# Neighbourhood attention with the transposed probabilities as stationary operand, and division by the denominators after the weighing

## Chip, core and metric

The kernel runs on one core of a Trainium2 chip. The metric is the device time of one execution in microseconds; the time before is the median of three runs. TensorE (PE) multiplies, with a separate record for its loads of stationary data (PEld); VectorE (DVE), ScalarE (ACT) and GpSimd (POOL) do the elementwise work; SyncE (SP) issues most of the transfers.

## What is computed

One layer of a hybrid encoder: an input projection, a state-space mixer, a neighbourhood attention over a 16 x 64 grid of tokens, an output projection and an MLP, all in float32. The change touches the attention alone. Cut to it, the reference is:

```python
def neighbourhood_attention(q, k, v, q_norm_w, k_norm_w, rpb):
    ...
    s = jnp.einsum("bjhd,bajchd->bhjac", q_i, k_win) + bias
    p = jax.nn.softmax(s.reshape(bsz, NA_HEADS, GRID_W, kh * NA_COLS), axis=-1)
    ...
    return jnp.einsum("bhjac,bajchd->bjhd", p, v_win)
...
x = x + jnp.concatenate([y_ssm, y_na], axis=-1) @ w_out
```

There are 1024 tokens, 16 heads of 64 dimensions, and a window of 8 rows by 16 columns.

## The kernel before

The tokens are put in 8 blocks of 128 (16 rows by 8 columns), so that the window of a block of queries lies in its own block of keys and the two beside it. Float32 products are made of halves: a value is split into a high part in fp32r and a remainder, and products of the parts are summed.

The attention runs over 8 pairs of heads, and in a pair over two heads (`attend`). For each of the 8 blocks b of queries it does this:

- Two matmuls (lines 931 and 934) put the scores of the block against up to three key blocks in a PSUM bank (`psc`, of two). q is stationary, with its high and low part stacked in the partitions; k moves, 256 or 384 columns.
- One DVE instruction (line 939) adds the bias with the mask (`mb`) and gives the row's maximum (`nmx`). ACT takes the exponential and sums it into the denominator `den` (line 949).
- DVE takes the reciprocal of the denominator (line 957) and multiplies the row by it (line 958).
- PE transposes the two or three pieces of 128x128 (line 962) into a bank `ptp` (of two), and ACT and DVE split them into `pth` and `ptl` (lines 184 and 185, `split_from_psum`).
- Three blocks later, `weigh(g)` multiplies key block g: v of that block, with its high and low part side by side (128 columns), is stationary, and the transposed probabilities of up to three query blocks move (line 908). Query blocks 0 to 3 sum into bank `pv0`, 4 to 7 into `pv1`. There are 20 such matmuls a head: 8 of 384 columns, 8 of 256, 4 of 128.
- After the last one of a bank, ACT copies the lower half of its partitions into the grid order (`yT`, line 918), and DVE adds the upper half (line 919).

After a pair, `yT` (128 dimensions by 1024 tokens) is stored to `na_dr` (line 996). At the start of the last pair, three earlier pairs are loaded again and split (lines 986 to 991); the last pair's output is split from `yT` itself (line 999).

Between the blocks stand fillers: the output projection of three quarters of its inner dimension (`w_out_part`, lines 178 to 180 as `po`), in pieces of 12 matmuls of 512 columns, about one for three blocks. Their weights are split by ACT (line 148) and POOL (line 149). POOL also builds the bias tile of each head (line 881). The instructions of an engine run in the order in which a scheduler has put them; so do the transfers that SP issues.

Of the kernel before, what the change touches and what calls it, by code (L numbers as in the profile page):

```python
# [1 line left out]

# [1 line left out]

# [51 lines left out]
def hymba_block(  # L56
# [135 lines left out]
    def to_grid(dst, h):  # L192
        v = dst.rearrange("p (i b j) -> p b i j", b=8, j=8)
        return v[:, 4 * h : 4 * h + 4]

    def from_blocks(src):
        return src.rearrange("p (b i j) -> p b i j", b=4, j=8)
# [575 lines left out]
    with ExitStack() as ph:  # L773
# [18 lines left out]
        def w_out_part(part, yt):  # L792
            for f in range(4 * part + len(yt), 4 * part + 4):
                yl = yp.tile([P, T], F32R, tag="yl", name="yl", bufs=4)
                yh = yp.tile([P, T], F32R, tag="yh", name="yh", bufs=4)
                yf = yl.bitcast(F32)
                if f < 8:
                    nc.sync.dma_start(
                        yf.rearrange("p (c f) -> p c f", c=NT),
                        y_dr[:, :, f * P : (f + 1) * P].rearrange("c p f -> p c f"),  # L800
                    )
                    pts = []
                    for h in range(2):
                        pt = ps_tp("pty")
                        for j in range(4):
                            c = 4 * h + j
                            nc.tensor.transpose(
                                pt[:, j * P : (j + 1) * P], yf[:, c * P : (c + 1) * P], ident
                            )
                        pts.append(pt)  # L810
                    for h in range(2):
                        s = slice(h * 512, (h + 1) * 512)
                        split_from_psum(
                            yh[:, s], yl[:, s], pts[h], pcol[:, 72 + f : 73 + f]
                        )
                else:
                    nc.sync.dma_start(yf, na_dr[f - 8])
                    split_na(yh, yl, yf, nc.gpsimd)
                yt.append((yh, yl))
            for h, t in ((h, t) for h in range(2) for t in range(NT)):  # L820
                if t == 0:
                    get = load_w_nat(w_out[0], 512 * part, 4, 512 * h, nc.gpsimd)
                pt = ps_mm("po")
                s = slice(t * P, (t + 1) * P)
                for k in range(4):
                    yh, yl = yt[k]
                    mm3(pt, yh[:, s], yl[:, s], *get(k), k == 0, k == 3)
                d = x2[:, t, h * 512 : (h + 1) * 512]
                if part == 0:
                    nc.sync.dma_start(  # L830
                        d, x[0, t * P : (t + 1) * P, h * 512 : (h + 1) * 512]
                    )
                nc.vector.tensor_tensor(d, d, pt, op=add)
                yield
# [54 lines left out]
        pth = ap.tile([P, NT, 3, P], F32R, name="pth", bufs=1)  # L889
        ptl = ap.tile([P, NT, 3, P], F32R, name="ptl", bufs=1)  # L890

        def attend(hh, mb, q, k, kl, v, yT):
            hp = slice(HD * hh, HD * hh + HD)
            nmx = ap.tile([P, 8], F32, tag="nmx", name="nmx")
            den = ap.tile([P, 8], F32, tag="den", name="den")
            pv = [ps_v("pv0"), None]

            def weigh(g):
                b0, b1 = max(g - 1, 0), min(g + 2, NT)
                for i in range(2):  # L900
                    c0, c1 = max(b0, 4 * i), min(b1, 4 * i + 4)
                    if c0 >= c1:
                        continue
                    first, last = g == 3 * i, g == 4 + 3 * i
                    if first and i:
                        pv[1] = ps_v("pv1")
                    for pt in (pth, ptl):
                        pvm = nc.tensor.matmul(
                            pv[i][:, (c0 - 4 * i) * P : (c1 - 4 * i) * P],
                            lhsT=v[:, g, hh],  # L910
                            rhs=pt[:, g, c0 - g + 1 : c1 - g + 1, :],
                            start=first and pt is pth,
                            stop=last and pt is ptl,
                            skip_group_check=True,
                        )
                    if last:
                        yo = to_grid(yT[hp], i)
                        nc.scalar.copy(yo, from_blocks(pv[i][0:HD]))
                        nc.vector.tensor_tensor(
                            yo, yo, from_blocks(pv[i][HD:P]), op=add  # L920
                        )
                return pvm

            for b in range(NT):
                g0, g1 = max(b - 1, 0), min(b + 2, NT)
                m = g1 - g0
                n = m * P
                o = (3 if b == 0 else 5 if b == NT - 1 else 0) * P
                qs, ks = slice(b * P, (b + 1) * P), slice(g0 * P, g1 * P)
                pt = ps_s("psc")  # L930
                nc.tensor.matmul(
                    pt[:, 0:n], lhsT=q[:, hh, qs], rhs=k[:, hh, ks], start=True, stop=False
                )
                mark = nc.tensor.matmul(
                    pt[:, 0:n], lhsT=q[:, hh, qs], rhs=kl[:, hh, ks], start=False, stop=True
                )
                pr = ap.tile([P, 384], F32, tag="pr", name="pr", bufs=4)
                db = den[:, b : b + 1]
                nc.vector.tensor_tensor_reduce(  # L939
                    pr[:, 0:n],  # L940
                    pt[:, 0:n],
                    mb[:, o : o + n],
                    scale=-1.0,
                    scalar=3.0e38,
                    op0=add,
                    op1=ALU.min,
                    accum_out=nmx[:, b : b + 1],
                )
                nc.scalar.activation(
                    pr[:, 0:n],  # L950
                    pr[:, 0:n],
                    AF.Exp,
                    bias=nmx[:, b : b + 1],
                    scale=-1.0,
                    accum_out=db,
                )
                nc.vector.reciprocal(db, db)
                nc.vector.tensor_scalar(pr[:, 0:n], pr[:, 0:n], db, None, op0=mul)
                pp = ps_tp("ptp")
                for j in range(m):  # L960
                    s = slice(j * P, (j + 1) * P)
                    nc.tensor.transpose(pp[:, s], pr[:, s], ident)  # L962
                s0 = 2 * g0 + b + 1
                hi, lo = (
                    t.rearrange("p g s q -> p (g s) q")[:, s0 : s0 + 2 * m - 1 : 2, :]
                    for t in (pth, ptl)
                )
                pv3 = pp[:, 0:n].rearrange("p (j q) -> p j q", q=P)
                split_from_psum(hi, lo, pv3)
                if b > 2:  # L970
                    weigh(b - 3)
                done[0] += 1
                if done[0] * 44 // 128 > (done[0] - 1) * 44 // 128:
                    with tc.issue_after(mark.ins):
                        fill()
            weigh(NT - 3)
            weigh(NT - 2)
            return mark, weigh(NT - 1)

        filler += [w_out_part(0, []), w_out_part(1, []), w_out_part(2, [])]  # L980
        last = []
        fill(2)
        for p in range(8):
            q, k, kl, v = load_qkv(p)
            if p == 7:
                for j, tag in enumerate(("q", "k", "v")):
                    hl = b0.tile([P, 2, T], F32R, tag=tag, name="hl", bufs=1)
                    yf = hl[:, 1].bitcast(F32)
                    nc.sync.dma_start(yf, na_dr[4 + j])
                    split_na(hl[:, 0], hl[:, 1], yf, nc.gpsimd)  # L990
                    last.append((hl[:, 0], hl[:, 1]))
            yT = yt.tile([P, T], F32, tag="yT", name="yT", bufs=1)
            for hh in range(2):
                marks = attend(hh, bias_for(2 * p + hh), q, k, kl, v, yT)
            if p < 7:
                nc.sync.dma_start(na_dr[p], yT)
            else:
                hl = b0.tile([P, 2, T], F32R, tag="kl", name="hl", bufs=1)
                split_na(hl[:, 0], hl[:, 1], yT, nc.vector)
                last.append((hl[:, 0], hl[:, 1]))  # L1000
        for i in (0, 1):
            with tc.issue_after(marks[i].ins):
                fill()
# [391 lines left out]
```

## Time and profile before

| | |
|---|---|
| median of 3 runs | 1684.91 us |
| lowest, highest | 1677.66, 1690.37 us |
| profiled execution, span from first to last instruction | 1676.4 us |
| attention, first to last weighing matmul | 689.2 to 964.5 us |
| mean granted PE clock | 0.986 |

The profile describes one execution, and the span above is the time that it gives for that execution. A row of a group has the line, the engine, the operation, output and inputs, partitions x elements and the count; then the busy time in us and the mean of one in ns; then how long the engine stood idle just before, and what ended that. A row of the stretch table has the busy time of each engine between two times. In the order of time, a row has the start and the duration in us, and xN says that N instructions in a row are merged. A PE matmul's duration contains its way through the array; the next one starts before it ends.

### The profile page before, as it was taken

The numbers are of one execution on the slowest core, as the hardware profiler recorded it, in microseconds if no ns is written. First come the engines' busy times: TensorE is split into PE (matmuls) and PEld (weight loads), VectorE is DVE, ScalarE is ACT, GpSimd is POOL, SyncE is SP. The second block draws the span as 40 slices with busy tenths as digits, with TensorE's granted clock in tenths as the row PEclk, the third lists the DMA queues.
The fourth block names the chain that finished last, engine by engine and source line by source line (L and its number), as shares of the span: only waits on it lengthen the run. The fifth ranks groups of instructions, "written<-read, shape, count | busy, mean of one in ns | idle before, by whom it ended". The sixth has DMA issues, their size and how long they took to land. (4 is left out here: it accounts for less than half of the span.)

```text
span 1676.4 us, 20931 instructions
## 1 busy us (share of the span) xinstructions
PE 1590.8 (95%) x7453; PEld 1297.3 (77%) x7453; DVE 1106.0 (66%) x1686; ACT 721.3 (43%) x1187; POOL 708.4 (42%) x506
## 2 busy tenths in 40 slices
PE   6999999998988899998999989999999989999999
PEld 5788888777766678887778767788888868888887
DVE  5767214788796852888898867544243387887863
ACT  5434223434343442556565533554444444433330
POOL 4000003888687862322243232244444465455551
PEclk9999999999999999999999999999999989999999
DMA  8113337876666785956664141353344386644231
GB/s 217 51 38 105 93 100 212 215 194 196 229 220 173 218 263 190 281 165 185 180 190 118 62 164 50 101 201 126 138 164 150 127 295 231 216 149 151 101 101 75
DMA packets 178755, 269.75 MB, mean 161 GB/s; under 512 B 14219, under 2 KB 105307, under 8 KB 178651
## 3 DMA queue, kind: packets, MB, share of 16 engines
q1 hardware_dynamic: 134667, 227.51, 44.1%
q10 hardware_dynamic: 42976, 37.23, 7.3%
q0 software_dynamic: 1008, 3.67, 0.5%
q8 instruction: 59, 0.97, 0.3%
q14 instruction: 45, 0.37, 0.1%
HBM read 185.21 MB, written 86.50 MB: 162 GB/s over the span
## 5 line engine op out<-in xcount | busy, mean ns | idle before, releaser
L760 POOL TENSOR_TENSOR wl<-wraw,wh 128x1024 fp32r<-128x1024 f32 x110 | 298.5, 2724 | 318.4 <-ACT wh L759 297.1
L759 ACT ACTIVATE wh<-wraw 128x1024 fp32r<-128x1024 f32 x110 | 115.6, 1054 | 149.7 <-PE px L745 50.8
L745 PE MATMUL px<-wh,ahl 128*128 128x512 f32 x512 | 162.5, 395 | 3.3 <-ACT ahl L759 3.3
L179 PE MATMUL pq<-wl,hTh 128*128 128x512 f32 x384 | 153.6, 402 | 4.9 <-DVE wl L149 4.8
L178 PE MATMUL pq<-wh,hTh 128*128 128x512 f32 x384 | 154.4, 405 | 3.5 <-ACT wh L148 3.5
L745 PE MATMUL px<-h,wh 128*128 128x512 f32 x496 | 156.0, 396 | 1.4 <-DVE x L1078 1.4
L180 PE MATMUL pq<-wh,hTl 128*128 128x512 f32 x384 | 152.9, 399 | 0.0
L760 DVE TENSOR_TENSOR ahl<-ar,ahl 128x1024 fp32r<-128x1024 f32 x56 | 115.1, 2062 | 23.2 <-ACT ahl L759 22.1
L759 ACT ACTIVATE ahl<-ar 128x1024 fp32r<-128x1024 f32 x56 | 58.2, 1052 | 140.1 <-PE px L745 75.3
L745 PEld LDWEIGHTS px<-wh,ahl 128*128 128x128 f32 x512 | 97.0, 190 | 25.0 <-ACT ahl L759 3.7
L745 PEld LDWEIGHTS px<-h,wh 128*128 128x128 f32 x496 | 93.2, 188 | 24.0 <-ACT h L184 1.6
L149 DVE TENSOR_TENSOR wl<-wraw,wh 128x1024 fp32r<-128x1024 f32 x40 | 55.3, 1386 | 81.9 <-ACT wh L148 81.2
L745 PE MATMUL px<-wl,ahl 128*128 128x512 f32 x256 | 101.0, 395 | 0.0
L745 PE MATMUL px<-h,wl 128*128 128x512 f32 x248 | 98.1, 395 | 0.0
L881 POOL TENSOR_TENSOR mb<-braw,nam 128x256 f32<-128x256 f32 (+1 forms) x48 | 40.1, 863 | 131.1 <-DVE nmx L939 72.2
L179 PEld LDWEIGHTS pq<-wl,hTh 128*128 128x128 f32 x384 | 73.6, 192 | 23.1 <-DVE wl L149 8.6
L149 POOL TENSOR_TENSOR wl<-wraw,wh 128x1024 fp32r<-128x1024 f32 x18 | 43.0, 2401 | 110.5 <-ACT wh L148 110.5
L178 PEld LDWEIGHTS pq<-wh,hTh 128*128 128x128 f32 x384 | 74.0, 193 | 20.2 <-ACT wh L148 5.2
L184 ACT ACTIVATE pth<-ptp 128x384 fp32r<-128x384 f32 (+1 forms) x128 | 57.7, 455 | 73.1 <-PE ptp L962 72.5
L612 POOL TENSOR_TENSOR rb<-rb,c 128x512 f32<-128x512 f32 x64 | 77.0, 1223 | 20.4 <-DMA rb<-cum_dr 19.2
L180 PEld LDWEIGHTS pq<-wh,hTl 128*128 128x128 f32 x384 | 73.5, 191 | 15.0
L745 PE MATMUL pz<-h,wh 128*128 128x512 f32 x256 | 80.8, 396 | 0.8 <-DVE h L185 0.8
(268 smaller groups left out, 4211.4 us busy)
## 6 DMA issues: line engine op xcount, KB each, us to landing
ar<-act_dr SPq DMA_DIRECT2D x56, 512.0 KB, 3.7
act_dr<-cq SPq DMA_DIRECT2D x49, 512.0 KB, 3.2
wraw<-in_w_in_dram SPq DMA_DIRECT2D x44, 512.0 KB, 4.3
rb<-cum_dr SPq DMA_DIRECT2D x32, 512.0 KB, 7.2
wraw<-in_w_mlp_in_dram SPq DMA_DIRECT2D x32, 512.0 KB, 4.6
wraw<-in_w_mlp_out_dram SPq DMA_DIRECT2D x32, 512.0 KB, 5.2
q_dr<-hl ACTq DMA_DIRECT2D x64, 128.0 KB, 3.6
k_dr<-hl ACTq DMA_DIRECT2D x16, 512.0 KB, 5.3
```

Source lines behind the costliest of these rows:

```text
L149: lo_eng.tensor_tensor(lo[:, 0:n], raw[:, 0:n], hi[:, 0:n].bitcast(F32), op=sub)
L178: nc.tensor.matmul(pt, lhsT=ah, rhs=bh, start=first, stop=False)
L179: nc.tensor.matmul(pt, lhsT=ah, rhs=bl, start=False, stop=False)
L180: return nc.tensor.matmul(pt, lhsT=al, rhs=bh, start=False, stop=last)
L184: nc.scalar.activation(hi, src, AF.Copy)
L612: nc.gpsimd.tensor_tensor(rb[:, d], rb[:, d], c1[:, d, c, h0 : h0 + 4].unsqueeze(2).broadcast_to([P, 4, P]), op=sub,)
L745: nc.tensor.matmul(pt, lhsT=a, rhs=b, start=f, stop=l, skip_group_check=True)
L759: nc.scalar.activation(hl[0], src, AF.Copy)
L760: eng.tensor_tensor(hl[1], src, hl[0].bitcast(F32), op=sub)
L881: nc.gpsimd.tensor_tensor(mb[:, s].rearrange("p (s r c) -> p s r c", r=16, c=8), v[:, a:b], nam[:, s].rearrange("p (s r c) -> p s r c", r= ...
```

## The change

The operands of the weighing change places: a 128x128 piece of `pth` or `ptl` (keys by queries) is stationary, and v moves. For each pair of key block and query block there are two matmuls: `pth` with v's high and low part (128 columns), and `ptl` with v's high part alone (64 columns). A head has 22 such pairs, so 44 matmuls. The bank then holds queries by dimensions.

Since queries are now in the partitions, the probabilities are not normalised any more: the lines of the reciprocal and of the product are gone, and the output is divided. When a bank is complete, DVE takes the reciprocal of four denominators at once, ACT copies the part from v's low half out of PSUM, DVE adds the other, and POOL multiplies by the reciprocals into `yn` (queries by both heads of the pair). The part of `ptl` with v's low half was computed before and is not any more.

`turn_out` brings the pair's output back to dimensions by tokens: 8 transposes, and a copy by ACT for each four (for the last pair a split by ACT and DVE). It is called in block 3 of the next pair's first head, so the store to `na_dr` moves there too, and for the seventh pair the three loads and splits follow it. The scratch area of software DMA is set to 4096 bytes.

```diff
-                for i in range(2):
-                    c0, c1 = max(b0, 4 * i), min(b1, 4 * i + 4)
...
-                    for pt in (pth, ptl):
-                        pvm = nc.tensor.matmul(
-                            pv[i][:, (c0 - 4 * i) * P : (c1 - 4 * i) * P],
-                            lhsT=v[:, g, hh],
-                            rhs=pt[:, g, c0 - g + 1 : c1 - g + 1, :],
...
+                for c in range(b0, b1):
+                    i = c // 4
...
+                    nc.tensor.matmul(
+                        pv[i][:, c0 : c0 + P],
+                        lhsT=pth[:, g, c - g + 1, :],
+                        rhs=v[:, g, hh],
...
+                    pvm = nc.tensor.matmul(
+                        pv[i][:, c0 : c0 + HD],
+                        lhsT=ptl[:, g, c - g + 1, :],
+                        rhs=v[:, g, hh, 0:HD],
...
-                        yo = to_grid(yT[hp], i)
-                        nc.scalar.copy(yo, from_blocks(pv[i][0:HD]))
-                        nc.vector.tensor_tensor(
-                            yo, yo, from_blocks(pv[i][HD:P]), op=add
+                        parts = pv[i].rearrange("p (b a d) -> p b a d", a=2, d=HD)
+                        bs = slice(4 * i, 4 * i + 4)
+                        nc.vector.reciprocal(den[:, bs], den[:, bs])
+                        yo = ap.tile([P, 4, HD], F32, tag="yo", name="yo")
+                        nc.scalar.copy(yo, parts[:, :, 1])
+                        nc.vector.tensor_tensor(yo, yo, parts[:, :, 0], op=add)
+                        nc.gpsimd.tensor_tensor(
+                            yn[:, bs, hh],
+                            yo,
+                            den[:, bs].unsqueeze(2).broadcast_to([P, 4, HD]),
+                            op=mul,
                         )
...
-                nc.vector.reciprocal(db, db)
-                nc.vector.tensor_scalar(pr[:, 0:n], pr[:, 0:n], db, None, op0=mul)
...
+                if b == 3 and late:
+                    late.pop()()
...
+        def turn_out(p, yn):
+            yf = hl = None
+            if p < 7:
+                yf = yt.tile([P, T], F32, tag="yT", name="yT", bufs=1)
+            else:
+                hl = b0.tile([P, 2, T], F32R, tag="kl", name="hl", bufs=1)
+            for h in range(2):
+                pt = ps_tp("pty")
+                for j in range(4):
+                    nc.tensor.transpose(
+                        pt[:, j * P : (j + 1) * P],
+                        yn[:, 4 * h + j].rearrange("p a d -> p (a d)"),
+                        ident,
+                    )
+                if p < 7:
+                    nc.scalar.copy(to_grid(yf, h), from_blocks(pt))
+                else:
+                    hi, lo = to_grid(hl[:, 0], h), to_grid(hl[:, 1], h)
+                    split_from_psum(hi, lo, from_blocks(pt))
+            if p < 7:
+                nc.sync.dma_start(na_dr[p], yf)
+            else:
+                last.append((hl[:, 0], hl[:, 1]))
+            if p == 6:
...
+            yn = yt.tile([P, NT, 2, HD], F32, tag="yn", name="yn", bufs=1)
             for hh in range(2):
-                marks = attend(hh, bias_for(2 * p + hh), q, k, kl, v, yT)
...
+            late.append(partial(turn_out, p, yn))
+        late.pop()()
...
+    nc = bacc.Bacc(
+        "TRN2", target_bir_lowering=False, num_devices=1, dynamic_dma_scratch_size=4096
+    )
```

Since lines were added, the changed kernel's lines have other numbers; in `attend` 931, 934, 939 and 962 are now 945, 948, 953 and 974, and earlier in the file each is one higher (184 and 185 are 185 and 186, 881 is 882). The order is seen at two places. The first is PE in the first head, in the blocks between two fillers; `psc` are the scores, `ptp` the transposes, `pv` the weighing. Before:

```order
L962 MATMUL ptp<-ident,pr 128x128 x3
L908 MATMUL pv_5598<-ptl,v 128x256
L908 MATMUL pv_5598<-pth,v 128x384
L962 MATMUL ptp<-ident,pr 128x128 x3
L908 MATMUL pv_5598<-ptl,v 128x384
L908 MATMUL pv_5598<-pth,v 128x384
L931 MATMUL psc<-k,q 128x384
L934 MATMUL psc<-kl,q 128x384
```

And in the changed kernel:

```order
L974 MATMUL ptp<-ident,pr 128x128 x3
L915 MATMUL pv_5598<-v,ptl 128x64
L907 MATMUL pv_5598<-v,pth 128x128
L915 MATMUL pv_5598<-v,ptl 128x64
L907 MATMUL pv_5598<-v,pth 128x128
L915 MATMUL pv_5598<-v,ptl 128x64
L907 MATMUL pv_5598<-v,pth 128x128
L945 MATMUL psc<-k,q 128x384
L948 MATMUL psc<-kl,q 128x384
```

Where one or two long matmuls stood between transposes and scores, a run of six short ones stands, each with stationary data of its own.

The second place is DVE in the same head, around the completion of the first bank. Before:

```order
L958 TENSOR_SCALAR pr<-pr,den 128x256
L957 RECIPROCAL den<-den 128x1
L185 TENSOR_TENSOR ptl<-ptp,pth 128x3x128
L958 TENSOR_SCALAR pr<-pr,den 128x256
L939 ISA pr,nmx<-psc,mb 128x384
L939 ISA nmx 128x1
L919 TENSOR_TENSOR yT<-yT,pv_5598 64x4x16x8
```

And in the changed kernel:

```order
L926 RECIPROCAL den<-den 128x4
L834 TENSOR_TENSOR x_5441<-x_5441,po 128x512
L953 ISA pr,nmx<-psc,mb 128x256
L953 ISA nmx 128x1
L186 TENSOR_TENSOR ptl<-ptp,pth 128x3x128
L953 ISA pr,nmx<-psc,mb 128x384
L953 ISA nmx 128x1
L186 TENSOR_TENSOR ptl<-ptp,pth 128x3x128
L953 ISA pr,nmx<-psc,mb 128x384
L953 ISA nmx 128x1
L929 TENSOR_TENSOR yo<-yo,pv_5598 128x256
```

Reciprocal and product of each block are gone from between the maxima and the splits; one reciprocal of four denominators stands for the bank, and the sum of the two parts keeps its place.

More of the change, by code (lines that the diff above doesn't have):

```diff
@@ L1 @@
 from contextlib import ExitStack
+from functools import partial
 import numpy as np
@@ L890, in hymba_block, with attend @@
         ptl = ap.tile([P, NT, 3, P], F32R, name="ptl", bufs=1)
-        def attend(hh, mb, q, k, kl, v, yT):
-            hp = slice(HD * hh, HD * hh + HD)
+        def attend(hh, mb, q, k, kl, v, yn, late):
             nmx = ap.tile([P, 8], F32, tag="nmx", name="nmx")
@@ L899, in weigh @@
                 b0, b1 = max(g - 1, 0), min(g + 2, NT)
-                for i in range(2):
-                    c0, c1 = max(b0, 4 * i), min(b1, 4 * i + 4)
-                    if c0 >= c1:
-                        continue
-                    first, last = g == 3 * i, g == 4 + 3 * i
+                for c in range(b0, b1):
+                    i = c // 4
+                    first = g == 3 * i and c == max(b0, 4 * i)
                     if first and i:
                         pv[1] = ps_v("pv1")
-                    for pt in (pth, ptl):
-                        pvm = nc.tensor.matmul(
-                            pv[i][:, (c0 - 4 * i) * P : (c1 - 4 * i) * P],
-                            lhsT=v[:, g, hh],
-                            rhs=pt[:, g, c0 - g + 1 : c1 - g + 1, :],
[L912 to L915, printed above, removed]
-                    if last:
-                        yo = to_grid(yT[hp], i)
-                        nc.scalar.copy(yo, from_blocks(pv[i][0:HD]))
-                        nc.vector.tensor_tensor(
-                            yo, yo, from_blocks(pv[i][HD:P]), op=add
@@ new lines, in weigh @@
+                    c0 = (c - 4 * i) * P
+                    last = g == 4 + 3 * i and c == min(b1, 4 * i + 4) - 1
+                    nc.tensor.matmul(
+                        pv[i][:, c0 : c0 + P],
+                        lhsT=pth[:, g, c - g + 1, :],
+                        rhs=v[:, g, hh],
+                        start=first,
+                        stop=False,
+                        skip_group_check=True,
+                    )
[3 more added lines that the diff above has]
+                        rhs=v[:, g, hh, 0:HD],
+                        start=False,
+                        stop=last,
+                        skip_group_check=True,
+                    )
@@ L978, in attend @@
             return mark, weigh(NT - 1)
[L980 to L985, printed above, removed]
+        def turn_out(p, yn):
[11 more added lines that the diff above has]
+                        ident,
+                    )
+                if p < 7:
[8 more added lines that the diff above has]
+            if p == 6:
                 for j, tag in enumerate(("q", "k", "v")):
@@ L991, in hymba_block @@
                     last.append((hl[:, 0], hl[:, 1]))
-            yT = yt.tile([P, T], F32, tag="yT", name="yT", bufs=1)
-            for hh in range(2):
-                marks = attend(hh, bias_for(2 * p + hh), q, k, kl, v, yT)
[L995 to L1000, printed above, removed]
+        filler += [w_out_part(0, []), w_out_part(1, []), w_out_part(2, [])]
+        last = []
+        late = []
+        fill(2)
+        for p in range(8):
+            q, k, kl, v = load_qkv(p)
+            yn = yt.tile([P, NT, 2, HD], F32, tag="yn", name="yn", bufs=1)
+            for hh in range(2):
+                marks = attend(hh, bias_for(2 * p + hh), q, k, kl, v, yn, late)
+            late.append(partial(turn_out, p, yn))
+        late.pop()()
         for i in (0, 1):
@@ L1379 @@
     from concourse.bass_utils import run_bass_kernel_spmd
-    nc = bacc.Bacc("TRN2", target_bir_lowering=False, num_devices=1)
+    nc = bacc.Bacc(
+        "TRN2", target_bir_lowering=False, num_devices=1, dynamic_dma_scratch_size=4096
+    )
     arrays, args = {}, []
```

## The prediction

> **What bounds the kernel now.** I read the page first (span, busy shares), then the stretch table, then the groups and waits of the attention stage, because that is the only stage whose instructions the change touches.
>
> ```profile
> span 1676.4 us, 20931 instructions
> PE 1590.8 (95%) x7453; PEld 1297.3 (77%) x7453; DVE 1106.0 (66%) x1686; ACT 721.3 (43%) x1187; POOL 708.4 (42%) x506
> core 0: us, PE busy (x) PEld busy (x) DVE busy (x) ACT busy (x) POOL busy (x), PEclk, DMA share, GB/s
> 690.00:965.00 275.00, 260.34 (x1453) 220.72 (x1453) 239.74 (x697) 166.70 (x428) 75.77 (x59) 0.99 0.55 161
> ```
>
> Over the span TensorE (PE) is the bound. The second row is the attention stage, 275 us from the first to the last weighing matmul: there VectorE (DVE) works 239.7 us, 87%, nearly as much as PE seems to. PE's 260.3 is overstated, since a matmul's modelled end overlaps the next one. What PE really needs must be counted from start to start. Next, the single matmuls of one stretch, the densest run of small matmuls, and the groups of the stage:
>
> ```profile
> 757.17 0.39 PE L178 MATMUL po<-wh,yh 128*128 128x512 f32 x1
> 757.40 0.39 PE L179 MATMUL po<-wl,yh 128*128 128x512 f32 x1
> 762.20 0.28 PE L908 MATMUL pv<-pth,v 128*128 128x256 f32 x1
> 762.32 0.28 PE L908 MATMUL pv<-ptl,v 128*128 128x256 f32 x1
> 762.44 0.22 PE L908 MATMUL pv<-pth,v 128*128 128x128 f32 x1
> 762.50 0.27 PE L908 MATMUL pv<-ptl,v 128*128 128x128 f32 x1
> 762.61 0.51 PE L962 MATMUL ptp<-ident,pr 128*128 128x128 f32 x3
> 763.19 0.34 PE L931 MATMUL psc<-k,q 128*128 128x384 f32 x1
> 763.37 0.33 PE L934 MATMUL psc<-kl,q 128*128 128x384 f32 x1
> 432.93 1.89 PE L630 MATMUL pd<-xs,rb 128*128 128x64 f32 x16
> L178 PE MATMUL po<-wh,yh 128*128 128x512 f32 x173 | 68.7, 397 | 0.0
> L962 PE MATMUL ptp<-ident,pr 128*128 128x128 f32 x344 | 59.2, 277 | 3.5 <-DVE den L957 2.4 <-DVE ptl L185 1.0
> L931 PE MATMUL psc<-k,q 128*128 128x384 f32 x90 | 35.7, 396 | 7.5 <-DVE nmx L939 7.5
> L931 PE MATMUL psc<-k,q 128*128 128x256 f32 x30 | 10.5, 350 | 1.5 <-DVE nmx L939 1.4
> L908 PE MATMUL pv<-pth,v x160: 218/323/525, 689.2 to 964.4; 128*128 128x256 f32 x64, 128*128 128x384 f32 x64, 128*128 128x128 f32 x32
> L908 PE MATMUL pv<-ptl,v x160: 273/339/669, 693.2 to 964.5; 128*128 128x256 f32 x64, 128*128 128x384 f32 x64, 128*128 128x128 f32 x32
> L630 PE MATMUL pd<-xs,rb x256: 217/275/422, 281.9 to 599.7; 128*128 128x64 f32 x128
> ```
>
> From start to start: 512 columns 0.23 us, 384 0.18, 256 0.12. The 128-column ones follow each other at 0.06 (762.44 to 762.50), and the next then comes after 0.11. Sixteen matmuls of only 64 columns, each with stationary data of its own, take 1.89 us: less the modelled length of the last, (1.89 - 0.275) / 15 = 0.108 us each, as if they had 240 columns. So below some 240 columns a matmul with its own stationary load costs about 0.108; three transposes say the same ((0.51 - 0.277) / 2 = 0.116).
>
> PE's work in the stage: fillers (output projection) 3 x 173 x 0.23 = 119; transposes 344 x 0.108 = 37; scores 2 x (90 x 0.178 + 30 x 0.12) = 39; weighing 128 x 0.178 + 128 x 0.12 + 64 x 0.108 = 45; about 4 for the transposes of the fillers. Sum 244 us of 275. The clock takes 3 (0.99 granted), so PE stands about 28 us. What it stands for:
>
> ```profile
> PE psc L931 <- DVE nmx L939: 8.9, 8, 2.7
> PE ptp L962 <- DVE den L957: 2.4, 2, 1.9
> PE pv L908 <- ACT pth L184: 1.1, 2, 0.6
> PE ptp L962 <- DVE ptl L185: 1.0, 2, 0.6
> ```
>
> What else PE waited for comes to under 1 us. Of the 13.4 us shown 12.3 name DVE: PE waits for the row maxima, which free the score banks, and for the normalised probabilities. So PE (244) and DVE (240) are near balance, and the stage is longer than either.
>
> **What comes off DVE.**
>
> ```profile
> L957 DVE RECIPROCAL den<-den 128x1 f32<-128x1 f32 x126 | 19.1, 155 | 0.3
> L958 DVE TENSOR_SCALAR pr<-pr,den 128x384 f32<-128x384 f32 x96 | 45.6, 481 | 1.2
> L958 DVE TENSOR_SCALAR pr<-pr,den 128x256 f32<-128x256 f32 x31 | 22.5, 726 | 0.4
> L919 DVE TENSOR_TENSOR yT<-yT,pv 64x512 f32<-64x512 f32 x32 | 22.1, 691 | 4.5 <-ACT yT L918 3.6
> L185 DVE TENSOR_TENSOR ptl<-ptp,pth 128x256 fp32r<-128x256 f32 x32 | 13.3, 415 | 0.0
> L918 ACT COPY yT<-pv 64x512 f32<-64x512 f32 x32 | 18.5, 577 | 16.1 <-PE pv L908 12.8 <-DMA na_dr<-yT 2.8
> L184 ACT ACTIVATE pth<-ptp 128x256 fp32r<-128x256 f32 x32 | 12.1, 379 | 26.3 <-PE ptp L962 26.3
> L187 ACT ACTIVATE yh<-pty,pcol 128x512 fp32r<-128x512 f32 x9 | 6.2, 686 | 4.6 <-PE pty L807 4.6
> L881 POOL TENSOR_TENSOR mb<-braw,nam 128x256 f32<-128x256 f32 x28 | 21.2, 778 | 0.0
> ```
>
> These rows cover 680 to 985, so that all 32 half outputs are in. Gone: 19.1 + 45.6 + 22.5 + 22.1 = 109 us. New: 32 reciprocals of 128x4 at 0.155 = 5, and 32 sums of 128x256 out of PSUM at 0.415 (the L185 row, same size and source) = 13. Net -91: DVE falls to some 149 us. ACT: 32 copies go from 0.577 to about 0.379 (-6), 14 turned copies at 0.686 come (+10): 170, no bound. POOL: 32 multiplications at 0.778 = +25, to 101; no bound by its sum.
>
> **What comes onto PE.** Weighing now loads the probabilities as stationary data, so one load serves one pair of key block and query block: 22 pairs a head, two matmuls each (128 columns, then 64), times 16 heads = 704, where 320 were. At 0.108 each: 76, against 45: +31. The output's transposes, 8 pairs of heads x 8, at 0.108: +7. Sum **+38**. No trace shows these matmuls in this data type and order, so bounds: from below 0.085, the mean of 0.06 and 0.11 in the rows at 762.44, giving 60 + 5 - 45 = +20; from above the 256-column 0.12, giving 84 + 8 - 45 = +47. I take 0.108, since the 64-column run is nearest: short, each with its own load, sustained over sixteen.
>
> **What of PE's standing time comes back.** 0 to 28 us. Where DVE is named (12.3 of 13.4) I expect it to go, but scores still have two banks and the chain maximum, exponential, transpose, split stays; I take two thirds, **-18**.
>
> **Moved steps.** The store of a pair and, for the seventh pair, the three loads and splits of earlier output wait until block 3 of the next head. On SP the store now stands behind that head's bias load, and the next-but-one pair's q and k loads stand behind it. In the trace these come late enough:
>
> ```profile
> 721.17 0.54 SPq L996 DMA_DIRECT2D na_dr<-yT  x1
> 738.51 0.61 SPq L855 DMA_DIRECT2D k<-k_dr  x1
> 943.23 2.39 POOL L790 TENSOR_TENSOR hl<-hl 128x1024 fp32r<-128x1024 f32 x1 [12.84 <-ACT hl L789]
> ```
>
> Between store and next q/k load lie 17 us, more than the four blocks of 2.1 us (275 / 128) by which the store moves; the last split ends at 946, and its first use comes after 965, the end of the stage. I cost both at 0; without that cover, up to 8 us for the pair. The multiplication on POOL is the new wait: behind it on POOL stand the next head's bias tile and the fillers' weight splits; PE waits for it at the turning, ACT when both buffers of the half output are full. The order gives it several blocks, so 0, with the price below. The smaller software-DMA area concerns only the seven POOL stores near 1355 us, and their readers come much later: 0, a few us if POOL blocks there.
>
> **Sum.** +38 - 18 = **+20 us**: the span of the profiled execution goes from 1676.4 to about 1696. That execution's span lies 8.5 under the median of the runs shown (1684.91) and near the lowest (1677.66), so on the median I predict **1705 us**, 1.2% slower. About 1%, 17 us, is what a measurement here can tell from no change.
>
> **Rivals.** (1) *Not slower: the loads hide.* If the load of one short matmul goes in under its neighbour, as the 0.06 step at 762.44 suggests, PE gains only 20 us of work and gets about as much standing time back: 20 - 18 = +2 or, with all 28 back, -8; about 1682 (1677 to 1690). Against it speaks the 64-column run at 0.108. Chance 0.2. The Trainium skill, "TensorE: Matmul & The Clock Gate", section "Back-to-back issue gap", gives some 81 ns a matmul sustained at 128 columns; by it the work would be 704 x 0.081 + 64 x 0.081 - 45 = +17, an estimate from that page, and the time unchanged. The trace disagrees, with 108 ns at 64 columns.
>
> (2) *Faster: DVE alone was the bound.* If every short matmul takes 0.06 (42 + 4 - 45, about +1) and all 28 us come back, the stage shrinks to some 248 and the median is near 1658. It decides only if short matmuls average under 0.085; the pairs of 0.06 are always followed by 0.11. Chance 0.06.
>
> (3) *Much slower: the detour over POOL holds the ring.* POOL's instructions run in order, and it has stood long in the bias tile:
>
> ```profile
> POOL mb L881 <- DMA v<-v_dr: 39.4, 2, 23.8
> POOL wl L149 <- ACT wh L148: 51.6, 4, 14.1
> ```
>
> A multiplication queued behind such a wait is late; when it is later than one half-head (17 us / 2), the third copy on ACT waits, behind it the exponentials, and then PE. At 1.5 us a head that is +24, and 1684.9 + 20 + 24 = 1729. For it: 23.8 us in one wait. Against: these waits mostly end when the previous head's maxima are done, before its outputs exist. Chance 0.14.
>
> (4) *The change does not do what it says*: the scheduler could spread short matmuls among long ones. The order shows them still in runs of five to seven between scores and transposes, so chance 0.02, time as (1).
>
> **Chances and range.** Forecast 0.58 (its own range 1690 to 1722), rivals 0.2, 0.06, 0.14, 0.02. About 0.37 of the forecast's 0.58 lies above +1%, with rival 3 0.51 slower; rivals 1 and 4 and the rest of the forecast 0.43 within 1%; 0.06 faster. The range goes from the forecast with short matmuls cheap and most of the standing time back, 20 - 24 = -4, to dear matmuls and nothing back, +47: 1681 to 1732.
>
> **What would show it.** In the profile after: short weighing matmuls 0.105 to 0.12 apart in runs (rival 1: 0.085 or less); DVE in the stage near 150 us; PE's waits for the row maxima down from 8.9 to under 4; the stage near 295 us. Wrong would be: a stage of 275 or less, ACT waiting for POOL, or PE still standing 28 us.

## The result and the profile after

The changed kernel takes 1697.6 us (median of 5), the kernel before beside it 1682.9 us: a ratio of 1.0087, 95% interval 1.0061 to 1.0113. It is slower, by 14.8 us between the medians. That is less than the 1% which the prediction took as the least that can be told, but the interval lies above 1, and a second series gave 1.0083 (1.0057 to 1.0110). The forecast was 1705 us, 1.2% slower, in 1681 to 1732.

First the span and the busy times of the changed kernel, then its attention stage in the stretch table (PE, PEld, DVE, ACT, POOL, granted clock), and one line for each form of the new weighing matmul (least, median and greatest duration in ns):

```profile
span 1695.8 us, 21777 instructions
PE 1619.8 (96%) x7901; PEld 1337.3 (79%) x7901; DVE 1029.3 (61%) x1463; ACT 723.9 (43%) x1202; POOL 723.5 (43%) x538
687.00:987.00 300.00, 295.45 (x1922) 266.02 (x1920) 170.28 (x488) 169.92 (x444) 92.35 (x90) 0.98 0.54 154
L907 PE MATMUL pv<-v,pth x352: 220/306/454, 687.8 to 987.0; 128*128 128x128 f32 x176
L915 PE MATMUL pv<-v,ptl x352: 191/246/402, 691.4 to 987.1; 128*128 128x64 f32 x176
```

The stage went from 275.3 us (689.2 to 964.5) to 299.2 (687.8 to 987.0); DVE's work in it fell from 240 to 170, and PE carries 448 matmuls more. The span grew by 19.4 us, to within a microsecond of the 1696 that the sum had given. That this fits so closely is partly luck: the execution profiled before is the quickest of its five (1677.7 us, 5.2 under their median), the one profiled after is the median of its five. Between the medians the growth is 14.8 us, and 14.2 in the second series, so the forecast of +20 is some 5 us too much. The other 2 us by which 1705 is too high come from the reference: the median of three runs was 1684.9, that of five is 1682.9.

How dense the short matmuls stand, in the order of time:

```profile
882.26 0.28 PE L915 MATMUL pv<-v,ptl 128*128 128x64 f32 x1
882.38 0.31 PE L907 MATMUL pv<-v,pth 128*128 128x128 f32 x1
882.52 0.24 PE L915 MATMUL pv<-v,ptl 128*128 128x64 f32 x1
882.60 0.31 PE L907 MATMUL pv<-v,pth 128*128 128x128 f32 x1
882.74 0.24 PE L915 MATMUL pv<-v,ptl 128*128 128x64 f32 x1
882.82 0.31 PE L907 MATMUL pv<-v,pth 128*128 128x128 f32 x1
882.97 0.24 PE L915 MATMUL pv<-v,ptl 128*128 128x64 f32 x1
883.04 0.33 PE L974 MATMUL ptp<-ident,pr 128*128 128x128 f32 x1
```

Seven short matmuls start in 0.78 us: 0.111 each. The step after 64 columns is shorter than the one after 128 (0.08 and 0.14), but the pair takes 0.22. What PE and its loads (PEld) wait for in the stage now, and one row of POOL:

```profile
PE ptp L974 <- ACT yT L1009: 2.7, 1, 2.7
PEld psc L945 <- DVE nmx L953: 2.4, 6, 0.5
PE psc L945 <- DVE nmx L953: 1.2, 4, 0.3
PE pv L907 <- ACT pth L185: 0.5, 2, 0.3
POOL yn L930 <- DVE yo L929: 150.7, 26, 18.5
```

The wait for the row maxima is 1.2 us in PE's rows where it was 8.9. The rows of the loads show more of it, before as after: it is 2.4 us there now. Before, the two largest rows of the loads in the stage were these:

```profile
PEld psc L931 <- DVE nmx L939: 13.6, 21, 3.0
PEld ptp L962 <- issue: 5.9, 13, 2.0
```

("issue" is idle time for which the profile shows no cause.) One stop of 2.7 us is new: the second copy of a turned output stands on ACT behind a split that waits for a load. In its multiplications POOL waits for the sums of VectorE, 150.7 us in all; no row shows another engine waiting for POOL's product.

Counted as in the prediction, with 0.111 us for a short matmul, PE's work is now 284 us: fillers 119, transposes (those of the fillers with them) 42, scores 39, weighing 78, output transposes 6. The clock takes 6 (0.98), so PE stands 9 to 10 us, where it stood 28. Around the stop the granted clock is low in this execution:

```profile
880.00:920.00 40.00, 37.31 (x224) 33.98 (x223) 19.80 (x59) 21.95 (x57) 20.35 (x16) 0.87 0.59 184
```

At a clock of 0.87 these 40 us lose 5. In the profile of the second series the same stop is there with 1.9 us, the stretch around it (870 to 910 us) has 0.96, and the stage is 295.7 us.

### The profile page after: what moved, and what is told of

It is laid out like the page before. It is cut to its first block, busy times and chain, and to the rows that moved or that the text cites. A ratio compares the mean times of both kernels' runs of the same rounds, so it can differ in the third digit from the quotient of the medians.

```text
span 1695.8 us, 21777 instructions
## 1 busy us (share of the span) xinstructions
PE 1619.8 (96%) x7901; PEld 1337.3 (79%) x7901; DVE 1029.3 (61%) x1463; ACT 723.9 (43%) x1202; POOL 723.5 (43%) x538
## 5 line engine op out<-in xcount | busy, mean ns | idle before, releaser
L761 POOL TENSOR_TENSOR wl<-wraw,wh 128x1024 fp32r<-128x1024 f32 x110 | 297.4, 2715 | 315.2 <-ACT wh L760 299.7
L907 PE MATMUL pv<-v,pth 128*128 128x128 f32 x352 | 89.9, 297 | 0.6 <-ACT pth L185 0.5
L953 DVE CUSTOM_DVE_ANT_0 pr<-psc,mb 128x384 f32<-128x384 f32 (+1 forms) x128 | 66.1, 520 | 36.1 <-PE ptp L974 34.0
L930 POOL TENSOR_TENSOR yn<-yo,den 128x256 f32<-128x256 f32 x32 | 19.7, 615 | 153.8 <-DVE yo L929 153.8
```

The costliest lines, as they stand in the source:

```text
L761: eng.tensor_tensor(hl[1], src, hl[0].bitcast(F32), op=sub)
L907: nc.tensor.matmul(pv[i][:, c0 : c0 + P], lhsT=pth[:, g, c - g + 1, :], rhs=v[:, g, hh], start=first, stop=False, skip_group_check=True,)
L930: nc.gpsimd.tensor_tensor(yn[:, bs, hh], yo, den[:, bs].unsqueeze(2).broadcast_to([P, 4, HD]), op=mul,)
L953: nc.vector.tensor_tensor_reduce(pr[:, 0:n], pt[:, 0:n], mb[:, o : o + n], scale=-1.0, scalar=3.0e38, op0=add, op1=ALU.min, accum_out=nmx[ ...
```

## The experiments

Ratios are to the kernel before, run beside each on the same chip; they come from all runs of both, and can differ from the ratio of the medians. e1 to e8 ran on one chip, e9 and e11 on another, e12 and e13 on a third. Stage is from the first to the last weighing matmul of one profiled execution; standing time is the stage less PE's counted work and less what the clock took, good to 1 or 2 us. Some expectations below quote standing times by earlier counts (33 and 12 us, 39 and 16); the table counts all runs in one way.

| run | median us | ratio, 95% | stage us | PE stands us |
|---|---|---|---|---|
| before | 1680 to 1683 | 1 | 275.3 | 28 |
| changed kernel | 1697.6 | 1.0087 (1.0061 to 1.0113) | 299.2 | 9 |
| e8, changed kernel again | 1695.7 | 1.0083 (1.0057 to 1.0110) | 295.7 | 9 |
| e1, before, no division | 1672.5 | 0.9927 (0.9900 to 0.9954) | 261.0 | 17 |
| e2, operands swapped alone | 1705.0 | 1.0155 (1.0123 to 1.0186) | 305.7 | 16 |
| e3, low part with 128 columns | 1701.5 | 1.0116 (1.0099 to 1.0132) | 298.7 | 12 |
| e4, low part left out | 1686.9 | 1.0027 (1.0005 to 1.0048) | 285.5 | 38 |
| e7, low part twice | 1731.5 | 1.0298 (1.0267 to 1.0329) | 330.8 | 8 |
| e5, turned copies on VectorE | 1697.3 | 1.0093 (1.0069 to 1.0117) | 295.5 | 11 |
| e11, multiplication on VectorE | 1699.4 | 1.0116 (1.0101 to 1.0131) | 298.1 | 11 |
| e6, late division, v stationary | 1689.8 | 1.0041 (1.0023 to 1.0059) | 286.3 | 37 |
| e9, the same by a 4-byte store | 1840.3 | 1.0955 (1.0938 to 1.0973) | 435.1 | 118 |
| e12, stretched out, VectorE | 1743.5 | 1.0380 (1.0353 to 1.0408) | 335.6 | 63 |
| e13, stretched out, POOL | 1678.7 | 0.9982 (0.9965 to 0.9999) | 274.4 | 25 |

e8 is the changed kernel without any edit, in the series of e5, e6 and e7:

> The changed kernel once more, beside the runs of this call on the same chip: 1.0087 of before (1.0061 to 1.0113).

Its ratio repeats the first to 0.0004, and its stage is 3.5 us shorter, about what the lower clock had taken from the first.

### The relief alone and the swap alone

e1 takes the two normalising instructions from the kernel before:

```diff
-                nc.vector.reciprocal(db, db)
-                nc.vector.tensor_scalar(pr[:, 0:n], pr[:, 0:n], db, None, op0=mul)
```

> The kernel before without the reciprocal and the product on VectorE (lines 957 and 958); the weighing keeps its operands, so the division by the denominators is left out. TensorE's work stays at some 243 us of the stage, VectorE falls from 240 to some 152 us. If VectorE is what TensorE stands for, as the forecast says, the stage loses two thirds or more of its 28 us: 18 to 26 us, about 1660 (1654 to 1668). If TensorE's standing time has another cause, the time stays within 8 us of before (1675 to 1691).

e2 puts the same two lines into the changed kernel and takes the division from its output:

```diff
-                        nc.vector.reciprocal(den[:, bs], den[:, bs])
...
-                        nc.vector.tensor_tensor(yo, yo, parts[:, :, 0], op=add)
-                        nc.gpsimd.tensor_tensor(
...
+                        nc.vector.tensor_tensor(yn[:, bs, hh], yo, parts[:, :, 0], op=add)
...
+                nc.vector.reciprocal(db, db)
+                nc.vector.tensor_scalar(pr[:, 0:n], pr[:, 0:n], db, None, op0=mul)
```

> The changed kernel with the probabilities normalised per block on VectorE as before, and no reciprocal and no multiplication at the output: the operands change places alone. TensorE's work is that of the changed kernel (about 283 us in the stage), VectorE's some 230 us. The forecast's terms, +38 for the short matmuls and the transposes and no relief, give a stage near 315 us if all of the old standing time stays, less where TensorE is now the longer one by 50 us: 10 to 18 us above the changed kernel, 1708 to 1716. If the relief of VectorE is worth nothing beside the short matmuls, the time is that of the changed kernel, 1693 to 1702.

The stage of e1 in the stretch table (PE, PEld, DVE, ACT, POOL, clock) and its largest wait of the loads, then the same of e2:

```profile
688.50:949.50 261.00, 256.46 (x1454) 218.56 (x1455) 175.65 (x454) 166.13 (x428) 73.69 (x59) 1.00 0.60 170
PEld psc L931 <- DVE nmx L939: 7.6, 20, 1.1
```

```profile
685.00:991.00 306.00, 296.58 (x1921) 265.40 (x1919) 235.49 (x703) 171.21 (x444) 75.55 (x59) 0.98 0.53 150
PEld psc L938 <- DVE nmx L946: 7.4, 10, 2.4
```

e1: DVE falls to 176 and the stage by 14, of which 3 are the clock (1.00 here) and 11 standing time. DVE was a cause, but of 28 us standing 17 stay with DVE idle for a third of the stage. The expectation was too good: 10 us came off between the medians (8 to 17 by the ratio's interval), not 18 to 26, though neither did the time stay. The 17 us are many short waits: the rows of the loads in e1's stage add up to 13 us, over half of it still for the row maxima, 20 waits of which the longest is 1.1 us.

e2: with DVE as loaded as ever (235 us), the swap alone makes the stage 30 longer, with 40 us more work on PE. So 12 of the 28 us go away with no relief at all; that a PE which is busy for longer gives DVE the time to be ready is the plain reading, but no run tests it apart. Removing the normalisation on top of the swap brings 7 to 9 us between the medians (1705.0 to 1697.6 or 1695.7), less than the 10 to 18 expected. By the ratios it is 0.7%, as much as e1's relief alone. In standing time the relief takes 11 us alone (28 to 17) and 7 on top of the swap (16 to 9), so the two effects overlap by some 4 us, from one execution of each kernel. The loads' wait for the row maxima shows both at work: 13.6 us before, 7.6 with the relief alone, 7.4 with the swap alone, 2.4 with both.

In e1 and e2 the order of PE's instructions is nearly that of the kernel which they were made from. In e4 and e7 below the scheduler put them in another order (about half of them stand in the same sequence), so these two differ from the changed kernel in more than their matmuls.

### The price of a short matmul

e3 gives the 64-column matmuls 128 columns; e4 leaves them out; e7 issues them twice.

```diff
                     pvm = nc.tensor.matmul(
-                        pv[i][:, c0 : c0 + HD],
+                        pv[i][:, c0 : c0 + P],
                         lhsT=ptl[:, g, c - g + 1, :],
-                        rhs=v[:, g, hh, 0:HD],
+                        rhs=v[:, g, hh],
```

> The changed kernel with v's high and low part as moving data of the low probabilities too: 352 matmuls of 64 columns get 128. If a short matmul is bound by the load of its stationary data, 0.11 us either way, nothing changes (within 4 us of the changed kernel, 1694 to 1702). If it is bound by its columns, 64 more of them at 0.45 ns make 352 x 0.029 = +10 us (1707).

```diff
-                    pvm = nc.tensor.matmul(
-                        pv[i][:, c0 : c0 + HD],
-                        lhsT=ptl[:, g, c - g + 1, :],
...
```

> The changed kernel without the 352 matmuls of the low probabilities, which leaves that part of the product out (their split on VectorE stays). At 0.108 us each TensorE loses 38 us of work; it stays the longest engine of the stage with some 245 us against ACT's 170, so 30 to 38 us come off: 1660 to 1668. If a short matmul costs 0.06, 21 us come off: 1677.

```diff
+                    for twice in range(2):
+                        pvm = nc.tensor.matmul(
+                            pv[i][:, c0 : c0 + HD],
+                            lhsT=ptl[:, g, c - g + 1, :],
...
```

> The changed kernel with each of the 352 matmuls of the low probabilities issued twice, so that the low product counts double. Leaving them out was no clean price, since TensorE then stood 33 us instead of 12 for other engines; adding them keeps TensorE the longest. At 0.108 us each the stage grows by 38 us, about 1735 (1730 to 1738). At 0.06 it grows by 21, 1719. If the second load of the same data is skipped, by less.

e7 is the cleanest, since PE hardly stands in it. Beside the changed kernel in the same series (1695.7) it takes 35.8 us more, as expected, and its stage 35.1 more (330.8 against 295.7): 0.100 us for each of 352, net of some 4 us that PE stood less or the clock took less. The stages of e8, e7 and e3:

```profile
685.00:982.00 297.00, 293.13 (x1924) 263.80 (x1923) 170.74 (x489) 170.70 (x445) 92.33 (x90) 0.99 0.54 155
684.00:1015.00 331.00, 328.37 (x2271) 300.59 (x2270) 171.23 (x488) 173.36 (x444) 92.54 (x90) 1.00 0.47 139
686.00:986.00 300.00, 293.83 (x1924) 263.99 (x1923) 170.88 (x489) 170.59 (x445) 92.33 (x90) 0.99 0.55 153
```

In the order of time a group of three in e7 (128, 64 and 64 columns) takes 0.33 to 0.34, 0.112 each, although the last loads the same data again:

```profile
741.09 0.30 PE L907 MATMUL pv<-v,pth 128*128 128x128 f32 x1
741.23 0.36 PE L916 MATMUL pv<-v,ptl 128*128 128x64 f32 x2
741.42 0.31 PE L907 MATMUL pv<-v,pth 128*128 128x128 f32 x1
741.57 0.36 PE L916 MATMUL pv<-v,ptl 128*128 128x64 f32 x2
741.76 0.31 PE L907 MATMUL pv<-v,pth 128*128 128x128 f32 x1
```

e3 doubles the columns of half of them. Its stage, 298.7, is 3.0 us longer than e8's at the same clock, and about 2 of these are waits (its stop for the turned copy is 1.0 longer, and a filler waits 1.3 for a weight split); 10 us more by columns would have shown. Its median is 3.8 above that of the changed kernel's first series, with overlapping intervals. So the cost goes by the instruction with its own stationary load and hardly by columns, at 64 and at 128. Every matmul here has a load of its own, so no run tells whether the load takes the time or the issue of the pair.

e4 missed its expectation: 39 us of PE's work went, and only 11 us of time. The largest waits of e4, over its stage and the start of the next:

```profile
PEld pv L907 <- ACT pth L185: 18.2, 41, 0.6
PE pv L907 <- ACT pth L185: 7.1, 25, 0.4
PEld ptp L966 <- ACT yT L1001: 7.3, 11, 3.4
```

The loads of the probabilities now wait for ACT's split, 41 times, where in the changed kernel such waits came to 1.6 us; those of the transposes wait for the turned copies on ACT. So 39 us less work came with 29 us more standing. Two causes are possible, and no run separates them: without the low part PE has less work between the split and the load that waits for it, and the order of PE's instructions is another.

### The detour of the output

```diff
-                    nc.scalar.copy(to_grid(yf, h), from_blocks(pt))
+                    nc.vector.tensor_copy(to_grid(yf, h), from_blocks(pt))
```

> The changed kernel with the 14 copies of the turned output on VectorE, which stands 40% of the stage, instead of ACT. In the changed kernel's trace the second copy of the fifth pair stands on ACT behind a split that waits 2.9 us for a load of earlier output; the PSUM bank is late, TensorE stops 2.7 us, and the granted clock is then half for 10.2 us. If that is what it costs, 3 us (the stop) to 8 us (with the slower clock) come off against the changed kernel run beside it: 1690 to 1695. If the stop only moves to another instruction behind the same load, nothing changes.

```diff
-                        nc.gpsimd.tensor_tensor(
+                        nc.vector.tensor_tensor(
                             yn[:, bs, hh],
```

> The changed kernel with the multiplication by the reciprocals on VectorE instead of POOL. If the detour over POOL costs nothing, as the forecast's sum has it, the time stays within 3 us of the changed kernel (1692 to 1700; VectorE gets some 13 us more and has 120 us free). If POOL's queue holds up the outputs (rival 3), 5 us or more come off: 1691 or less.

Neither brings anything. In e5 the stop for the turned copy is gone, and a filler waits 1.0 us behind the same load instead; the time is 1697.3 against 1695.7 in the same series. So taking away the stop gains nothing that can be measured, and the stretch with the clock of 0.87 had 0.96 in the second profile. e11, on another chip, is if anything slower (1.0116): that POOL's queue holds up the outputs is refuted.

### The relief without the swap

With a loss from the swap and a gain from the relief, the next kernel keeps v stationary and divides late. The output then has queries along its columns, so the reciprocals must be spread over the partitions. e6 does it through memory:

```diff
+                nc.vector.reciprocal(den, den)
+                pd = ps_tp("pden")
+                nc.tensor.transpose(pd[0:8, 0:P], den, ident)
+                dn = ap.tile([8, P], F32, tag="dn", name="dn")
+                nc.scalar.copy(dn, pd[0:8, 0:P])
+                nc.sync.dma_start(den_dr[2 * p + hh], dn)
+                nc.sync.dma_start(
+                    rb[hp], den_dr[2 * p + hh].rearrange("b q -> (b q)").partition_broadcast(HD)
+                )
...
+                nc.gpsimd.tensor_tensor(
+                    yo, yo, from_blocks(rb[hp, 512 * i : 512 * i + 512]), op=mul
+                )
```

> The kernel before with v stationary as it was, but the division moved behind the weighing: per head one reciprocal of 128x8, one transpose to 8x128, a store and a load that spreads it over 64 partitions, and two multiplications of 64x512 on POOL in block 4 of the next head (the last head is normalised as before). It takes VectorE's relief without the short matmuls. The run without normalisation gave 0.9927 of before; 15 short transposes add 2 us to TensorE, and POOL gets 38 us that it has room for. If the relief can be had alone: 0.991 to 0.996 of before, 1668 to 1676. If the detour over the transfer or POOL's queue is late (the half output holds its buffer into the next pair), before or above: 1683 or more.

e6 is 0.4% slower than before. PE's work is as before but for 2 us; it stands 37 us, 20 more than in e1. Waits of e6 in the stage:

```profile
POOL yT L1004 <- DMA rb<-den_dr: 48.3, 8, 12.6
ACT dn L990 <- PE pden L988: 20.5, 10, 7.8
PEld psc L934 <- DVE nmx L942: 11.7, 29, 1.0
PEld pv L911 <- ACT pth L186: 10.0, 23, 3.7
PEld po L181 <- POOL wl L151: 4.1, 1, 4.1
```

POOL stands in its product until the load has landed, and behind it is a weight split for which PE waits once, 4.1 us. ACT stands for the transpose, and PE's loads wait 10.0 us for ACT's splits, where it was 2.7 in e1, and 11.7 for the row maxima (7.6 in e1). That ACT's standing causes these longer waits was not tested. Three variants try to get the queues out of the way. e9 stores the reciprocals as they lie and multiplies on VectorE (the edits of e9, e12 and e13 are shown against e6):

```diff
-                nc.tensor.transpose(pd[0:8, 0:P], den, ident)
...
-                nc.sync.dma_start(den_dr[2 * p + hh], dn)
+                nc.sync.dma_start(den_dr[2 * p + hh].rearrange("b q -> q b"), den)
...
-                nc.gpsimd.tensor_tensor(
+                nc.vector.tensor_tensor(
```

> Late division as in the run before it, with the engine queues out of the way: the reciprocals go to memory as they lie (4 bytes at a time), without transpose and ACT copy; the load that spreads them is issued in block 3 of the next head, when the store has landed; VectorE multiplies in block 5, not POOL. In the first late division TensorE stood 39 us against 16 without any division, and ACT (20 us for the transposed denominators), POOL (48 us for the load) and the filler's weight split behind POOL waited. If these queued waits made it slow, the stage comes to within 5 to 8 us of the 261 us without division, the time to 0.994 to 0.998 of before (1671 to 1678). If the 16 us of multiplication on VectorE, or the later store, cost as much again: 1.000 or more.

It is 9.5% slower. First the transfer itself (4 KB, 10.7 us from issue to landing), then SP's queue, then DVE, PE and the stage:

```profile
den_dr<-den SPq DMA_DIRECT2D x15, 4.0 KB, 10.7
```

```profile
SPq L995 <- DMA den_dr<-den: 149.9, 15, 12.9
```

```profile
DVE yT L1004 <- DMA rb<-den_dr: 157.2, 15, 14.1
PE psc L934 <- DVE nmx L942: 79.1, 11, 12.9
688.00:1124.00 436.00, 289.33 (x1458) 245.85 (x1457) 199.15 (x516) 169.24 (x430) 73.59 (x59) 0.83 0.51 112
```

4 KB in pieces of 4 bytes land after 10.7 us; SP waits 10.0 us for them each time before the spreading load, where in e6, with the same 4 KB in rows of 512 bytes, it waited 20.9 us in 14 waits. DVE waits for the spreading load, and behind DVE's product stand the row maxima and so PE. The clock is down to 0.83 on top.

e12 and e13 keep the transpose and spread the steps over the next head (transpose and store in block 1, load in block 3, product in block 6); e12 has the product on VectorE, e13 on POOL.

```diff
-                if b == 4 and late:
+                if b in (1, 3, 6) and late:
...
                 late.append(partial(divide, p, hh, yT))
+                late.append(partial(spread, p, hh))
+                late.append(partial(to_row, p, hh, den))
```

> Late division with v stationary, stretched out over the next head: the reciprocals are transposed and stored in block 1, spread by a load in block 3, and VectorE multiplies in block 6, so that no queue stands for a transfer. VectorE keeps some 67 of its 88 us of relief (30 products of 64x512 at 0.684 us cost 20). If the lag takes the waits away, the stage is some 266 us, 5 over the one without division, and the time 0.993 to 0.998 of before (1669 to 1677). If the chain through SP still holds VectorE in some heads: 0.999 to 1.006.

> The same with the products on POOL, 1.29 us each, 38 us in all. If POOL's order keeps the fillers' weight splits waiting behind products, as in the first late division, 0.999 to 1.005 of before; if the lag is enough, VectorE keeps all of its relief and the time is 0.992 to 0.997 (1667 to 1676).

Both missed what was expected: e12 is 3.8% slower, and e13 at 0.9982 lies just outside both of its ranges. The lag did not suffice. First the waits of e12, then those of e13 with its stage:

```profile
DVE yT L1011 <- DMA rb<-den_dr: 46.3, 15, 8.9
PE pv L911 <- DVE ptl L187: 16.7, 4, 6.5
```

```profile
POOL yT L1011 <- DMA rb<-den_dr: 59.8, 11, 14.4
688.00:963.00 275.00, 265.32 (x1472) 222.48 (x1471) 183.07 (x486) 169.06 (x444) 111.74 (x89) 0.99 0.64 177
```

Three blocks are 6 to 8 us at the lengths of these stages, and the landing times of the spreading load that the traces give are 11.4 us (e12) and 10.5 (e13). The products wait on POOL at least as long as on VectorE (59.8 and 46.3 us), but behind VectorE's queue stand the maxima and the splits of every block; in e13 no wait of PE in the stage names POOL. The two runs differ in the engine of the product alone. e13 is 0.9982 of before (0.9965 to 0.9999): about 1% under the changed kernel, and hardly distinguishable from before. Of the relief of e1 (0.9927), a quarter is left.

## Why the prediction was right

**Direction and size.** Slower was forecast, by 1.2%; it is 0.9%. The prediction's own bound of 1% runs between the two, so by its chances the outcome fell among the 0.43 within 1%, not the 0.51 slower. That the span grew by 19.4 us where +20 was forecast is partly luck, as said above: between the medians it is 14 to 15. In the stage itself the sum holds: PE's work +40, standing time -19 and the clock, which the prediction had left as it was, +3 make +24 (275.3 to 299.2); in e8's profile, where the clock took no more than before, it is +20. The rest of the profiled execution was 4.5 us shorter than before, which nothing in the change explains.

**The term for PE, +38.** Right, by the cause that was given: 0.111 measured for 0.108, so +33 for the weighing and +6 or 7 for the transposes, about +40. e7's added matmuls and e3's added columns show that it goes by the instruction. The row chosen from a different stage, 64 columns with a load of their own, was the right neighbour; the rivals that built on the 0.06 step (1 and 2) fall with it. Rival 4 falls too: the short matmuls stand in runs, as the order had them. The figure of 81 ns a matmul, from the Trainium skill's "TensorE: Matmul & The Clock Gate", section "Back-to-back issue gap", is not borne out for these operands.

**The term for the standing time, -18.** Right in sum, 28 to 9 or 10, and only half right in its reason. The prediction put it down to DVE's relief. e2 shows 12 us of it gone with DVE fully loaded; the relief adds the other 7. e1 shows the relief alone at 11. So each change alone takes away less than two thirds, and the -18 came out because the swap, which the prediction had counted only as a cost, took away standing time as well. This is the step that failed as an explanation. The rows that it was read from told half of the story: PE's rows showed 13.4 us of waits and the prediction had "under 1 us" besides, but the rows of the loads (PEld) add up to 26 of the 28 us, 13.6 for the row maxima and 5.9 with no cause shown. In e1, e2 and the changed kernel they give 13 of 17, 14 of 16 and 8 of 9. The standing time is read from the loads.

**DVE's work.** 149 was forecast, 170 measured, and e1's relief was 64 us of busy time where the rows removed had 87. The durations of DVE's instructions in the trace can overlap the next one's, so a sum of groups is more than the engine's time: DVE's rows of before add up to 279 us in a stretch where its busy time is 240. By that share the 91 us are 13 too many; the other 8 were not traced.

**Moved steps and POOL at 0.** Not contradicted. Rival 3 is refuted by e11 and by POOL's wait for its inputs, and e5 gains nothing. A new stop of 2.7 us (1.9 in the second profile) did come, which the prediction did not have. The store, the reloads and the software DMA area were not tried apart.

**What stays open.** Why the loads still wait 7.6 us for the row maxima in e1, with DVE idle for a third of the stage. The prediction's remark that two score banks and the chain of maximum, exponential, transpose and split stay fits it; no run changed the banks or the chain.

## What to carry to other kernels

Count a small matmul by the instruction with its own stationary load, not by its columns: swapping operands so that the small side moves turned 320 matmuls into 704 and cost PE 40 us, more than the relief of another engine could give back. When two engines are nearly balanced, removing work from one is worth what a run with only that removal shows: here 10 us for 64 us of VectorE's time. Beside a longer PE the same removal took away less standing time, 7 us against 11. Read what PE waits for from its loads as well as from its matmuls; here the matmuls' rows showed half of it. A late step whose input comes through memory belongs on the engine behind which nothing urgent is queued.

## What the runs showed of the hardware beyond what was expected

A matmul that loads the same stationary data as the one before it is no cheaper: 0.112 us in e7. A wait for the moving data shows at the stationary load too: in e6 v is stationary, and yet the loads of the weighing stood 10.0 us, 23 times, until ACT's split of the probabilities that move. A store of 4 KB in pieces of 4 bytes took 10.7 us to land in e9. Long standing went with a low clock: with PE standing about 118 us of a 435 us stage in e9 the granted clock was 0.83, with 63 of 336 us in e12 it was 0.92, against 0.99 before.
